# Attention's first loads and looks inside the last projections, and DVE alone for the sums of weights in the short sequence

## The chip, the core and the metric

The kernel runs on one core of a Trainium2 chip. The metric is the device time of one launch in microseconds, taken over several runs; beside it stands one execution taken by the hardware profiler, from which all rows of the profile come. TensorE is PE (its weight loads PEld), VectorE is DVE, ScalarE is ACT, GpSimd is POOL, and SyncE is SP. In this kernel SP issues every transfer.

## The reference

Two sequences, "prompt" with 1024 tokens and "sample" with 2048, go through one layer with shared weights. Everything is float32.

```python
h = rms_norm(x, norm_pre)
z = jnp.einsum('btd,de->bte', h, w_in)                    # 1024 -> 2304 columns
u_pool, g_pool, q, k, v, g_attn, q_x, g_x = jnp.split(z, SPLITS, axis=-1)
pool_out = multiscale_pool(u_pool, pool_w, pool_scale) * silu(g_pool)   # windows 2, 4, 8, 16
q = apply_rope(rms_norm(q, q_norm)); k = apply_rope(rms_norm(k, k_norm))
attn_out = block_self_attention(q, k, v) * silu(g_attn)   # 8 heads on 2 key heads, softmax over all tokens
k_m, v_m = split(rms_norm(mem, mem_norm) @ w_mem_kv)      # 256 memory tokens
x_out = memory_attention(q_x, k_m, v_m) * silu(g_x)       # 4 heads
y = concatenate([pool_out, attn_out, x_out]) @ w_out      # 1024 -> 1024
out = x + rms_norm(y, norm_post)
```

## The kernel before

**Phase 1, the projections.** `SB` lists what is projected: the memory, then the tokens in pieces of 1024 (two blocks of 512). For each piece six groups of weight columns run one after the other: queries (`group_n0`), a group of transposed chunks (`ct[2]`), queries, keys and values (`group_n1`), then three more groups of chunks, `ct[0]` (two pooling chunks and a gate), `ct[1]` (three gates) and `ct[3]` (a cross query and two gates). A product in float32 precision is made of three matmuls of high and low halves (L139 to L141, tile `pz`), eight times over the 1024 inputs, so 24 matmuls a tile. Results are staged in SBUF and stored to scratch in HBM: `dq`, `dqx` (queries), `dk`, `dv`, `dkm`, `dvm` (keys and values), `dg` (gates), `dp` (pooled input). A pooling chunk (`pool_chunk`) is windowed on POOL (tiles `s2`, `s4`, `sm`), multiplied with `poolw` on PE (`pm`, L332), scaled on DVE into `s4` again (L334), and stored from `s4` to `dp`. There is one `s4`, so the next chunk's second window sum, which writes it, waits for that store.

**Phase 2, the attention.** A pair is 256 queries; the 8 pairs of "sample" come first, then the 4 of "prompt". A pair has three groups: two of self-attention (kind 0 and 1, over 16 or 8 chunks of 128 keys) and one of cross-attention (kind 2, two chunks). The work is written out as a list of slots, one for each chunk of each group, and the order on PE, ACT, DVE and POOL is that of this program; SP's order is left to the scheduler. In a slot stand:

- `weights`: scores `S` of the chunk for two halves of the lanes (L595, L599: keys `KA` with query `qa`, then `KB` with `qb`, whose 65th row carries minus the maximum), and exp on ACT into `P` (L602).
- `sums`: adds the previous chunk's `P` into `z`, columns 0 to 511 on POOL, 512 to 1023 on DVE (L613, `CUT` = 512).
- `largest`, here called a look: scores `N` of 128 queries against up to 1024 keys (L567, L559), and a maximum over them on DVE (L570), for a group that starts at least four slots later. `N` has two buffers. After a group's last look, `shift` transposes the maxima (L504) and stores them as the row of `qb` (L584).
- `values`: every four chunks, `acc` += `P` times `V` (L625). After a group's last chunk `totals` multiplies `z` with a tile of ones in four quarters (L633), `take` multiplies `acc` with the gate, `inverse` takes the reciprocal (L645) and spreads it over partitions through HBM (`rows`, `gz`).
- `store_mix` multiplies (POOL, L661) and splits into high and low half (`mix`; ACT and POOL, L784); `Output.piece` is the output projection (L726 to L728, tile `py`, for the last pair `N`), spread over the next pair's slots. `Output.out` multiplies with the norm (L752) and adds the residual `xr` (L755). `xr` and `y` have one buffer each.

Since nothing of the first groups has been looked at when phase 2 begins, 20 looks stand ahead of its first slot: 16 of the second group, 2 of the first (cross-attention), 2 of the third. All tiles of phase 2 are taken when those of phase 1 have been given back.

Of the kernel before, what the change touches and what calls it, by code (L numbers as in the profile page):

```python
# [23 lines left out]
def encoder(ctx, tc, I, O):  # L24
# [46 lines left out]

    with ExitStack() as p1:
# [3 lines left out]
        pst = p1.enter_context(tc.tile_pool(name="pst", bufs=2, space=PSUM))  # L76
# [15 lines left out]
        def hT_block(sb, blk):  # L92
# [4 lines left out]
            for i in range(4):  # L97
                x = two.tile([128, D], F32, name="x", tag="x", bufs=4)
                nc.sync.dma_start(out=x, in_=rows(sb, blk, i))
                if kind not in gains:  # L100
                    gains[kind] = one.tile([128, D], F32, name="gain", tag="gain")
                    src = I["mem_norm" if kind == "mem" else "norm_pre"]
                    nc.sync.dma_start(out=gains[kind], in_=src.broadcast_to([128, D]))
                junk = one.tile([128, D], mybir.dt.bfloat16, name="junk", tag="junk")
                ss = two.tile([128, 1], F32, name="ss", tag="ss")
                nc.scalar.activation(out=junk, in_=x, func=AF.Square, accum_out=ss)
                r = rsqrt(two, ss, 1, D, "rsx")
# [27 lines left out]
        def product(ps, terms):  # L135

            n = len(terms)
            for c, (sh, sl, mh, ml) in enumerate(terms):
                nc.tensor.matmul(ps, lhsT=sh, rhs=mh, start=c == 0, stop=False)  # L139
                nc.tensor.matmul(ps, lhsT=sh, rhs=ml, start=False, stop=False)  # L140
                nc.tensor.matmul(ps, lhsT=sl, rhs=mh, start=False, stop=c == n - 1)  # L141

# [9 lines left out]
        def transposed(hT, w, col):  # L152

            ps = psz.tile([128, 512], F32, name="pz", tag="pz")
            f = slice(col, col + 128)
            product(ps, [(w[0][:, c, f], w[1][:, c, f], hT[0][:, c], hT[1][:, c]) for c in range(NC)])
            return ps
# [4 lines left out]
        def rope_tables():  # L162
            out = []
            raw = [two.tile([128, NTT, 64], F32, name="ropec", tag="ropec", bufs=1),
                   two.tile([128, NTT, 64], F32, name="ropes", tag="ropes", bufs=1)]
            for r, key in zip(raw, ("rope_c", "rope_s")):
                nc.sync.dma_start(out=r, in_=I[key])
            for key in ("k_norm", "q_norm"):
                g = one.tile([128, 2, 64], F32, name="hg", tag="hg" + key)
# [9 lines left out]
                for j in range(2):  # L179
                    if key == "q_norm":  # L180
                        t = raw[j]
                    else:
                        t = one.tile([128, NTT, 64], F32, name="ropek", tag=f"ropek{j}")
# [7 lines left out]
        def norm_rope(ps, parts, tt):  # L191
# [3 lines left out]
            z = two.tile([128, 384], F32, name="z", tag="z")  # L195
            sq = two.tile([128, 384], F32, name="sq", tag="sq")
            t1 = two.tile([128, 384], F32, name="t1", tag="t1")
            nc.scalar.copy(out=z[:, 0:w], in_=ps[:, 0:w])
            nc.scalar.activation(out=sq[:, 0:w], in_=ps[:, 0:w], func=AF.Square)
            ss = two.tile([128, 6], F32, name="ssh", tag="ssh")  # L200
# [3 lines left out]
            r = rsqrt(two, ss[:, 0:n], n, 64, f"rsh{n}")  # L204
# [22 lines left out]
        def heads_transposed(src, npair):  # L227
# [4 lines left out]
            o = two.tile([128, 2, 3, 128], F32R, name="qst", tag="qst")  # L232
# [20 lines left out]
        def group_n1(s, b, hT, w):  # L253
            for i in range(4):
                tt = 4 * b + i
                ps = natural(hT, w, i, 0, 384)
                vst = two.tile([128, 2, 64], F32, name="vst", tag="vst")
# [104 lines left out]
        def chunks_group(chunks):  # L362
            def run(s, b, hT, w):
                for k, (_, f, args) in enumerate(chunks):
                    f(s, b, *args, transposed(hT, w, 128 * k))
# [25 lines left out]
        def mem_v(s, b, hT, w):  # L391
            for i in range(4):
                ps = natural(hT, w, i, 0, 256).rearrange("p (h d) -> p h d", d=64)
                vst = two.tile([128, 4, 64], F32, name="vmst", tag="vmst", bufs=1)
# [15 lines left out]

        for sb, (kind, s, nb, b0) in enumerate(SB):
            groups = groups_of(sb)
            nxt = []
            for gi, (src, pieces, run) in enumerate(groups):
# [15 lines left out]
    with ExitStack() as p2:  # L430
        def pool(name, bufs, space=bass.MemoryType.SB):
            return p2.enter_context(tc.tile_pool(name=name, bufs=bufs, space=space, reuse_waits="tile"))

        one = pool("p2one", 1)
        two = pool("p2two", 2)
        pss = pool("pss", 2, PSUM)
        psn = pool("psn", 2, PSUM)
        psa = pool("psa", 1, PSUM)
        pso = pool("pso", 1, PSUM)

        ones = one.tile([128, 32], F32, name="ones")
        nc.vector.memset(ones, 1.0)

        KA = [one.tile([128, 2048], F32R, name=f"KA{kind}") for kind in range(2)]
        KB = [one.tile([128, 2048], F32R, name=f"KB{kind}") for kind in range(2)]
        KA.append(one.tile([128, 2, 2, NMEM], F32R, name="KA2"))
        KB.append(one.tile([128, 2, 2, NMEM], F32R, name="KB2"))
        for t in KB:  # L450
            nc.vector.memset(t[64:65].bitcast(F32), 1.0)
        V = [one.tile([128, 16, 64], F32, name=f"V{kind}") for kind in range(2)]
        V.append(one.tile([128, 2, 4, 64], F32, name="V2"))
        has_K, has_V = set(), set()

        def load_K(s, kind):
            has_K.add((s, kind))
            for hl in range(2):
                for t, h in ((KA, 64 * hl), (KB, 0))[:2 - hl]:
                    if kind == 2:  # L460
                        src = DKM[hl, :, :, s].rearrange("d (c j) m -> d c j m", j=2)
                        nc.sync.dma_start(out=t[2][h:h + 64].bitcast(F32), in_=src)
                        continue
                    for a in range(0, SEQS[s][1], 1024):
                        nc.sync.dma_start(out=t[kind][h:h + 64, a:a + 1024].bitcast(F32),
                                          in_=DK[s][kind][hl, :, a:a + 1024])

        def load_V(s, kind):
            has_V.add((s, kind))
            if kind == 2:  # L470
                nc.sync.dma_start(out=V[2], in_=DVM[s])
                return
            for a in range(0, SEQS[s][1] // 128, 8):
                nc.sync.dma_start(out=V[kind][:, a:a + 8], in_=DV[s][kind][:, a:a + 8])

        wo_hi = one.tile([128, NC, D], F32R, name="wo_hi")
        wo_lo = one.tile([128, NC, D], F32R, name="wo_lo")
        raws = {}

        def load_w_out(c):  # L480
            raws[c] = two.tile([128, D], F32, name="raw", tag=("y", "xr")[c % 2], bufs=1)
            nc.sync.dma_start(out=raws[c], in_=I["w_out"][0, 128 * c:128 * c + 128])

        def split_w_out(c):
            raw = raws.pop(c)
            nc.scalar.copy(out=wo_hi[:, c], in_=raw)
            nc.gpsimd.tensor_tensor(out=wo_lo[:, c], in0=raw, in1=wo_hi[:, c].bitcast(F32), op=ALU.subtract)

        npost = one.tile([128, D], F32, name="npost")

        def load_npost():
            nc.sync.dma_start(out=npost, in_=I["norm_post"].broadcast_to([128, D]))


        lanes32 = {}
        for name in ("top",):
            lanes32[name] = [one.tile([128, 32], F32, name=f"{name}{n}") for n in range(2)]
            for t in lanes32[name]:
                nc.vector.memset(t, 0.0)

        def lanes_to_rows(t, name):

            r = two.tile([128, 32], F32, name="rows32", tag=f"r{name}")
            nc.vector.transpose(out=r, in_=t)  # L504
            return r

        BASE = (2, 4, 6)

        class Group:

            def __init__(self, n, s, p, kind):
                self.n, self.s, self.p, self.kind = n, s, p, kind
                T = SEQS[s][1]
                self.chunks = 2 if kind == 2 else T // 128
                self.parts = 1 if kind == 2 else T // 1024
                self.pieces = [(0, j) for j in range(2)] if kind == 2 else \
                    [(a, lane) for a in range(self.parts) for lane in range(8)]
                self.P = {}  # L520

            def load(self):
                s, p, kind = self.s, self.p, self.kind
                if (s, kind) not in has_K:
                    load_K(s, kind)
                self.qa = one.tile([128, 2, 512], F32R, name="qa", tag="qa", bufs=4)
                for h in range(2):
                    self.load_q(self.qa[64 * h:64 * h + 64], 0)
                self.top = lanes32["top"][self.n % 2]
                if self.parts > 1:  # L530
                    self.nb = two.tile([128, self.parts, 8], F32, name="nb", tag="nb")

            def load_q(self, out, hl):
                s, p = self.s, self.p
                src = DQX[s, p // 2][hl, p % 2].rearrange("d j c q -> d j (c q)") if self.kind == 2 else \
                    DQ[s, p, self.kind][hl].rearrange("d j t i q -> d j (t i q)")
# [221 lines left out]

        CUT = 512


# [156 lines left out]
```

## Time and profile before

| | |
|---|---|
| median of 3 runs | 1941.95 us (1940.56 to 1943.42) |
| profiled execution | 1940.45 us, span 1938.6 us |
| granted TensorE clock, mean | 0.974 |
| PE / DVE / POOL / ACT busy | 1830.0 / 1126.4 / 914.3 / 699.3 us |
| phase 1, first to last projection matmul | up to 691.8 us |
| first score matmul | 746.2 us |
| short sequence's sums | about 1608 to 1895 us |

A busy engine isn't always at its peak, so what a stage waits for is read from the rows: a timeline row gives the start, the length, the engine and line, what is written from what, how often, and in brackets the idle time before it with the event that ended it. A row of the chain of waits gives start, length and what held the end. A row of waits gives who waited for whom: total, times, longest.

### The profile page before, as it was taken

The numbers are of one execution on the slowest core, as the hardware profiler recorded it, in microseconds if no ns is written. First come the engines' busy times: TensorE is split into PE (matmuls) and PEld (weight loads), VectorE is DVE, ScalarE is ACT, GpSimd is POOL, SyncE is SP. The second block draws the span as 40 slices with busy tenths as digits, with TensorE's granted clock in tenths as the row PEclk, the third lists the DMA queues.
The fourth block names the chain that finished last, engine by engine and source line by source line (L and its number), as shares of the span: only waits on it lengthen the run. The fifth ranks groups of instructions, "written<-read, shape, count | busy, mean of one in ns | idle before, by whom it ended". The sixth has DMA issues, their size and how long they took to land.

```text
span 1938.6 us, 23683 instructions
## 1 busy us (share of the span) xinstructions
PE 1830.0 (94%) x8520; PEld 1289.7 (67%) x8520; DVE 1126.4 (58%) x1304; ACT 699.3 (36%) x1266; POOL 914.3 (47%) x816
## 2 busy tenths in 40 slices
PE   7999999999999938999999999999999999999995
PEld 6998898978998824456565655656565655565564
DVE  6833254422623018876767677676767666756742
ACT  5522242313422102543434444443434443333331
POOL 3735033620634003863746456373746454635644
PEclk9999999999999967899999999999999999999998
DMA  6653355434443273212112021222212143323211
GB/s 235 200 147 89 110 161 138 116 100 123 118 123 86 66 176 118 82 39 77 60 47 80 26 79 44 77 60 77 61 48 78 49 125 83 93 77 104 82 39 60
DMA packets 148486, 181.84 MB, mean 94 GB/s; under 512 B 21504, under 2 KB 118416, under 8 KB 148368
## 3 DMA queue, kind: packets, MB, share of 16 engines
q1 hardware_dynamic: 148368, 180.33, 32.6%
q8 instruction: 67, 1.10, 0.2%
q14 instruction: 51, 0.42, 0.1%
HBM read 126.50 MB, written 53.62 MB: 93 GB/s over the span
## 4 chain that ended last, share of the span: by engine, by line
PE 70%; issue 10%; DVE 8%; POOL 6%; DMA 4%; ACT 2%; SPq 1%; POOLq 0%; ACTq 0%; DVEq 0%
PE acc L625 13%; PE S L595 11%; PE pz L141 9%; PE pz L139 9%; PE pz L140 9%; PE N L567 6%; PE py L726 3%; PE py L727 3%; PE py L728 3%; DVE nb L570 2%; POOL z L613 2%; DVE z L613 2%; PE S L599 1%; POOL rs L63 1%; PE N L633 1%
## 5 line engine op out<-in xcount | busy, mean ns | idle before, releaser
L602 ACT ACTIVATE P<-S 128x512 f32<-128x512 f32 x688 | 401.3, 599 | 612.8 <-PE S L595 435.4
L613 POOL TENSOR_TENSOR z<-z,P 128x512 f32<-128x512 f32 x272 | 389.2, 1431 | 260.3 <-ACT P L602 253.9
L570 DVE TENSOR_REDUCE nb<-N 128x1 f32<-128x1024 f32 x256 | 311.0, 1218 | 229.0 <-PE N L567 228.2
L625 PE MATMUL acc<-P,V 128*64 128x512 f32 (+1 forms) x1472 | 318.2, 574 | 0.5
L595 PE MATMUL S<-qa,KA 128*128 128x512 f32 x640 | 277.3, 433 | 11.6 <-ACT P L602 11.5
L613 DVE TENSOR_TENSOR z<-z,P 128x512 f32<-128x512 f32 x272 | 262.2, 964 | 15.9 <-ACT P L602 15.4
L567 PE MATMUL N<-KA,qa 128*128 128x512 f32 x640 | 217.0, 423 | 46.1 <-DMA qa<-dq 29.5
L595 PE MATMUL S<-qb,KB 65*128 65x512 f32 x640 | 255.2, 399 | 0.0
L139 PE MATMUL pz<-hT_hi,w_hi 128*128 128x512 f32 x592 | 233.2, 394 | 2.6 <-ACT w_hi L68 1.8
L140 PE MATMUL pz<-hT_lo,w_hi 128*128 128x512 f32 x592 | 233.9, 395 | 0.0
L141 PE MATMUL pz<-hT_hi,w_lo 128*128 128x512 f32 x592 | 232.3, 392 | 0.0
L595 PEld LDWEIGHTS S<-qa,KA 128*128 128x128 f32 x640 | 121.7, 190 | 146.4 <-issue 71.9
L625 PEld LDWEIGHTS acc<-P,V 128*64 128x64 f32 x1472 | 98.1, 137 | 177.6 <-issue 168.5
L567 PEld LDWEIGHTS N<-KA,qa 128*128 128x128 f32 x640 | 119.3, 198 | 97.5 <-DVE nb L570 35.1
L63 POOL TENSOR_TENSOR rs<-rs,mhalf 128x1 f32<-128x1 f32 (+2 forms) x100 | 92.9, 932 | 175.7 <-DVE rs L61 175.5
L570 DVE TENSOR_REDUCE top<-N 128x1 f32<-128x1024 f32 (+1 forms) x88 | 107.1, 1218 | 109.5 <-PE N L567 79.6
L613 POOL TENSOR_TENSOR z<-P 128x512 f32<-128x512 f32 x36 | 46.6, 1294 | 215.4 <-ACT P L602 154.3
L140 PE MATMUL pz<-w_lo,hT_hi 128*128 128x384 f32 (+1 forms) x416 | 140.5, 338 | 0.9 <-DVE w_lo L69 0.8
L141 PE MATMUL pz<-w_hi,hT_lo 128*128 128x384 f32 (+1 forms) x416 | 140.2, 338 | 0.0
L139 PE MATMUL pz<-w_hi,hT_hi 128*128 128x384 f32 (+1 forms) x416 | 139.4, 336 | 0.0
L726 PE MATMUL py<-wo_hi,mix 128*128 128x512 f32 x352 | 138.0, 392 | 0.0
L727 PE MATMUL py<-wo_lo,mix 128*128 128x512 f32 x352 | 137.2, 390 | 0.0
(115 smaller groups left out, 2587.5 us busy)
## 6 DMA issues: line engine op xcount, KB each, us to landing
wraw<-w_in SPq DMA_DIRECT2D x15, 1536.0 KB
dg<-gst SPq DMA_DIRECT2D x48, 256.0 KB
qa<-dq SPq DMA_DIRECT2D x48, 256.0 KB
gz<-rows SPq DMA_DIRECT2D x72, 128.0 KB
x<-x_sample SPq DMA_DIRECT2D x16, 512.0 KB
xr<-x_sample SPq DMA_DIRECT2D x16, 512.0 KB
y_sample<-xr SPq DMA_DIRECT2D x16, 512.0 KB
dq<-qst SPq DMA_DIRECT2D x48, 128.0 KB
```

Source lines behind the costliest of these rows:

```text
L63: nc.gpsimd.tensor_tensor(out=r, in0=r, in1=mhalf[:, 0:n], op=ALU.pow)
L139: nc.tensor.matmul(ps, lhsT=sh, rhs=mh, start=c == 0, stop=False)
L140: nc.tensor.matmul(ps, lhsT=sh, rhs=ml, start=False, stop=False)
L141: nc.tensor.matmul(ps, lhsT=sl, rhs=mh, start=False, stop=c == n - 1)
L567: nc.tensor.matmul(S[:, 512 * b:512 * b + 512], lhsT=q, rhs=KA[self.kind][:, k:k + 512], start=True, stop=True)
L570: nc.vector.tensor_reduce(out=out, in_=S, axis=AX.X, op=ALU.max, negate=True)
L595: nc.tensor.matmul(S, lhsT=K[self.kind][rows_, keys], rhs=q, start=n == 0, stop=n == 1)
L602: nc.scalar.activation(out=self.P[k][:, j], in_=S, func=AF.Exp)
L613: e.tensor_tensor(out=z[:, x], in0=a[:, x], in1=P[:, x], op=ALU.add)
L625: nc.tensor.matmul(self.acc[64 * j:64 * j + 64, x], lhsT=v, rhs=P[:, j, x], start=(k, i) == (0, 0), stop=k == self.chunks - 1, skip_group_ ...
L726: nc.tensor.matmul(ps, lhsT=mh, rhs=wo_hi[:, c, cols], start=first, stop=False)
L727: nc.tensor.matmul(ps, lhsT=mh, rhs=wo_lo[:, c, cols], start=False, stop=False)
```

## The change

Three things change. The diff below is cut to them; most of the other changed lines only move the classes of phase 2 ahead of phase 1 and rename pools (`one` and `two` of phase 2 are now `own` and `dbl`; those tiles of phase 1 that aren't needed in its last three groups are in `fone` and `ftwo`, on the other side of SBUF). The quarters of ones in `totals` are the same in both.

1. After `group_n1` of the last piece, `fone` and `ftwo` are given back, and `early` takes their room: `KA`, two of three `KB`, queries, maxima. The first three groups are loaded there (`load`). After `ct[0]` the PSUM banks of phase 1's transposes go to `N`. In the last group (`ct[3]`) one look is written behind every second of a product's eight steps; PE's order is by hand there. `KB` is now loaded in `shift`, and `KB1` stays in the late pool.
2. `CUT` is 512 for "sample" and 0 for "prompt": there DVE adds all 1024 columns in one instruction, and POOL none.
3. In the last pair, `xr` and `y` of both tiles take buffers of `P` and are loaded before the first product.

```diff
+    def look_ahead():
+        if ahead:
+            g, n = ahead.pop(0)
+            g.largest(n)
...
-        def product(ps, terms):
+        def product(ps, terms, beside=lambda: None):
...
+                if c % 2:
+                    beside()
...
+                last = sb + 1 == len(SB)
+                if last and gi == 3:
+                    front.close()
+                    early = ctx.enter_context(tc.tile_pool(name="early", bufs=1, side="right", reuse_waits="tile"))
+                    open_early()
+                    for g in loads.pop(-1):
+                        g.load()
+                if last and gi == 4:
+                    heads.close()
+                    psn = ctx.enter_context(tc.tile_pool(name="psn", bufs=2, space=PSUM, side="right", reuse_waits="tile"))
...
-                    run(s, b0 + blk, cur[blk], w)
+                    if last and final:
+                        with tc.manual_schedule(engines={mybir.EngineType.PE}):
+                            run(s, b0 + blk, cur[blk], w, look_ahead)
+                    else:
+                        run(s, b0 + blk, cur[blk], w)
...
-            with tc.high_priority(offset=2000):
-                for g in loads.pop(-1):
-                    g.load()
-                for g, n in ahead:
-                    g.largest(n)
...
             def shift(self):
+            load_K(self.s, self.kind, KB, 0, 0)
...
-                for e, x in ((nc.gpsimd, slice(0, CUT)), (nc.vector, slice(CUT, 1024))):
-                    e.tensor_tensor(out=z[:, x], in0=a[:, x], in1=P[:, x], op=ALU.add)
+            cut = CUT[self.s]
+            if cut:
+                nc.gpsimd.tensor_tensor(out=z[:, :cut], in0=a[:, :cut], in1=P[:, :cut], op=ALU.add)
+            nc.vector.tensor_tensor(out=z[:, cut:], in0=a[:, cut:], in1=P[:, cut:], op=ALU.add)
...
-        CUT = 512
+    CUT = (0, 512)
...
-                self.xr = two.tile([128, D], F32, name="xr", tag="xr", bufs=1)
+            tag = dict(tag="P", bufs=6) if self.last else dict(tag="xr", bufs=1)
+            self.xr = dbl.tile([128, D], F32, name="xr", **tag)
...
                 if self.last:
                     if self.both is None:
+                    self.start()
```

How the order moves, first on SP, in the last piece between `group_n1` and the pooling chunks' stores. Before (`dk` keys, `dp` pooled input, `dg` a gate):

```order
L237 DMA dk_114<-qst 64x2x128
L338 DMA dp_112<-s_5394 128x512
L343 DMA dg_2_0_98<-gst 512x1x128
L338 DMA dp_112<-s_5433 128x512
L343 DMA dg_3_0_107<-gst 512x1x128
L338 DMA dp_112<-s_5503 128x520
```

And now (KA_5378, KA_5379, KA_5376 are the keys of kind 1, 2 and 0, KB_... their second copies):

```order
L648 DMA dk_114<-qst 64x2x128
L99 DMA KA_5378<-dk_114 64x1024 x4
L161 DMA qa<-dq_0_1_76 64x1024 x2
L96 DMA KA_5379<-dkm 64x4x256 x2
L161 DMA qa<-dqx_0_79 64x1024 x2
L99 DMA KA_5376<-dk_114 64x1024 x4
L161 DMA qa<-dq_0_0_75 64x1024 x2
L749 DMA dp_112<-s_5437 128x512
L754 DMA dg_2_0_98<-gst 512x1x128
L96 DMA KB_5380<-dkm 64x4x256
L161 DMA qb<-dqx_0_79 64x1024
L99 DMA KB_5377<-dk_114 64x1024 x2
```

Sixteen loads stand between the last store of keys and the first store of the pooled input, nine more behind it; before, all of them stood behind the last gate of phase 1.

On PE, the second pooling product `pm` of the same stage, before, at the start of the gate tile of `ct[0]`'s second block:

```order
L141 MATMUL pz_5517<-hT_hi_4214,w_lo_4906 128x512
L139 MATMUL pz_5563<-hT_hi_4214,w_hi_4905 128x512
L140 MATMUL pz_5563<-hT_lo_4215,w_hi_4905 128x512
L332 MATMUL pm_5441<-sm_5434,poolw_145 128x512
L141 MATMUL pz_5563<-hT_hi_4214,w_lo_4906 128x512
```

And now, in the second gate tile of `ct[1]`:

```order
L550 MATMUL pz_5672<-hT_hi_4038,w_lo_5366 128x512
L548 MATMUL pz_5672<-hT_hi_4038,w_hi_5365 128x512
L549 MATMUL pz_5672<-hT_lo_4039,w_hi_5365 128x512
L743 MATMUL pm_5484<-sm_5477,poolw_151 128x512
L550 MATMUL pz_5672<-hT_hi_4038,w_lo_5366 128x512
```

It stands 54 projection matmuls later than before.

On PE at the seam, before, from the last projection matmul to the first scores:

```order
L141 MATMUL pz<-hT_hi,w_lo 128x512
L567 MATMUL N<-KA_5966,qa 128x512 x28
L559 MATMUL N<-KA_5970,qa 128x256 x8
L567 MATMUL N<-KA_5966,qa 128x512 x4
L567 MATMUL N<-KA_5967,qa 128x512 x4
L599 MATMUL S<-qa,KA_5970 128x256 x2
L599 MATMUL S<-qb,KB_5971 128x256 x2
```

And now, first a place in the last projection group, then the seam itself:

```order
L191 MATMUL N<-KA_5376,qa 128x512 x2
L548 MATMUL pz<-hT_hi,w_hi 128x512
L549 MATMUL pz<-hT_lo,w_hi 128x512
L550 MATMUL pz<-hT_hi,w_lo 128x512
L548 MATMUL pz<-hT_hi,w_hi 128x512
L549 MATMUL pz<-hT_lo,w_hi 128x512
L550 MATMUL pz<-hT_hi,w_lo 128x512
L191 MATMUL N<-KA_5376,qa 128x512 x2
```

```order
L550 MATMUL pz<-hT_hi,w_lo 128x512
L224 MATMUL S<-qa,KA_5379 128x256 x2
L224 MATMUL S<-qb,KB_5380 128x256 x2
L191 MATMUL N<-KA_5378,qa 128x512 x2
L224 MATMUL S<-qa,KA_5379 128x256 x2
```

The 20 looks lie in the first five of the last group's six tiles; nothing but scores follows the last projection matmul.

More of the change, by code (lines that the diff above doesn't have):

```diff
@@ new lines, in due, with open_fill @@
+    def due(slot):
+        for f, args in later.pop(slot, ()):
+            f(*args)
+    first = {}
+    for n, (g, k) in enumerate(slots):
+        first.setdefault(g, n)
+    fill, until = [], [0]
+    def open_fill(pair, slot):
+        fill.extend(pair.todo())
+        n = pairs.index(pair) + 1
+        until[0] = first[pairs[n].groups[0]] + HOLD[pairs[n].s] if n < len(pairs) else slot
+    for pair in pairs:
+        ends = [first[g] + g.chunks - 1 for g in pair.groups]
+        at(min(ends), pair.load_pool)
+        free = 0 if pair is pairs[0] else first[pair.groups[0]] + HOLD[pair.s]
+        at(max(min(ends) + 4, free), pair.pool, max(min(ends) + 4, free))
+        for g in pair.groups:
+            wait = max(first[g] + g.chunks + 5, free)
+            at(wait + END, g.mix_out, wait + END, pair)
+        at(max(ends) + 9, open_fill, pair, max(ends) + 9)
@@ new lines, in encoder @@
+    for g in groups:
+        n, c = first[g], g.chunks
+        at(n + END, g.load_late)
+        for k in range(0, c, RUN):
+            ks = list(range(k, min(k + RUN, c)))
+            at(n + ks[-1] + 1 + END, g.values, ks)
+        at(n + c + 1 + END, g.totals)
+        at(n + c + 2, g.take)
+        at(n + c + 2 + END, g.inverse)
+    for c in range(NC):
+        at(4 + 3 * c, load_w_out, c)
+        at(7 + 3 * c, split_w_out, c)
+    at(7 + 3 * NC, load_npost)
+    looks, n = {}, len(slots)
@@ new lines, in encoder @@
+    left = {g: list(range(len(g.pieces))) for g in groups}
+    while any(left.values()):
+        n -= 1
+        able = [g for g in groups if left[g] and first[g] - LEAD > n]
+        if able:
+            looks[n] = (able[0], left[able[0]].pop())
+    ahead = [looks[n] for n in sorted(looks) if n < 0]
+    loads = {}
+    for n, (g, k) in looks.items():
+        if k == 0:
+            loads.setdefault(max(n - 3, -1), []).append(g)
+    order = {mybir.EngineType.PE, mybir.EngineType.Activation, mybir.EngineType.DVE,
+             mybir.EngineType.Pool}
@@ L182, in rope_tables @@
                     else:
-                        t = one.tile([128, NTT, 64], F32, name="ropek", tag=f"ropek{j}")
+                        t = fone.tile([128, NTT, 64], F32, name="ropek", tag=f"ropek{j}")
                     nc.gpsimd.tensor_tensor(out=t, in0=raw[j],
@@ new lines, in encoder @@
+    V.append(own.tile([128, 2, 4, 64], F32, name="V2"))
+    wo_hi = own.tile([128, NC, D], F32R, name="wo_hi")
+    wo_lo = own.tile([128, NC, D], F32R, name="wo_lo")
+    npost = own.tile([128, D], F32, name="npost")
+    with tc.manual_schedule(engines=order):
+        slot = 0
+        while slot < len(slots) or later or fill:
+            g, k = slots[slot] if slot < len(slots) else (None, 0)
+            if g:
+                g.weights(k, 0)
+            if 0 < slot <= len(slots):
+                h, kh = slots[slot - 1]
+                h.sums(kh)
+            for x in loads.get(slot, ()):
+                x.load()
+            if slot in looks:
+                looks[slot][0].largest(looks[slot][1])
+            due(slot)
+            if g:
+                g.weights(k, 1)
+            pauses = sum(x is None for x in fill)
+            n = -(-(len(fill) - pauses) // max(1, until[0] - slot - pauses)) if fill else 0
+            for _ in range(n):
+                x = fill.pop(0)
+                if x is None:
+                    break
+                out, h, c, start, final = x
+                out.piece(h, c, start, final)
+                if final:
+                    if h == 0 and not out.last:
+                        for n in sorted(later):
+                            for x in [x for x in later[n] if x[0].__name__ in ("square", "norm", "out")]:
+                                later[n].remove(x)
+                                x[0](*x[1])
+                    at(slot + END, out.half_out, h)
+                    at(slot + 1 + END, out.square, h)
+                    if h == 1:
+                        at(slot + 2, out.norm)
+                        at(slot + 3, out.out)
+            due(slot + END)
+            slot += 1
```

690 lines of the change are left out of this document (305 added, 385 removed).

## The prediction

> **What bounds the kernel now.** I read the page's slices of time first, then the windows by stage, the chain of waits at the seam between the two phases, and last the waits of PE in the short sequence and at the end. In the windows the columns after the stage and its length are the busy time (and count) of PE, PEld, DVE, ACT and POOL, then PE's granted clock, the DMA engines' share and GB/s.
>
> ```profile
> PE   7999999999999938999999999999999999999995
> 600.00:691.80 91.80, 91.77 (x400) 74.25 (x399) 17.31 (x23) 12.57 (x18) 12.78 (x13) 1.00 0.23 70
> 691.80:721.20 29.40, 0.00 (x0) 0.00 (x0) 0.00 (x0) 1.88 (x2) 0.00 (x0) 0.55 0.98 207
> 721.20:746.20 25.00, 23.03 (x44) 11.38 (x45) 22.34 (x22) 0.00 (x0) 0.00 (x0) 0.50 0.68 198
> 1730.00:1810.00 80.00, 75.38 (x346) 49.47 (x347) 50.68 (x53) 29.71 (x57) 43.11 (x30) 0.98 0.34 98
> ```
>
> PE is the bound nearly everywhere; the "3" in its slices is the seam. There PE does nothing for 29.4 us while the DMA engines are 98% busy, and then works at half its clock (0.50) for 25 us. In the 91.8 us before, PE is full, DVE has 17 us of work and the DMA engines are 77% free.
>
> ```profile
> 691.54 0.24 PE pz L141
> 711.46 9.73 DMA qa<-dq
> 721.23 1.24 PE N L567 x2
> 722.49 1.24 DVE nb L570
> 746.24 0.63 PE L599 MATMUL S<-qa,KA 128*128 128x256 f32 x2
> 751.06 0.63 PE L567 MATMUL N<-KA,qa 128*128 128x512 f32 x2
> 751.53 0.40 PE L595 MATMUL S<-qa,KA 128*128 128x512 f32 x1
> 752.09 1.95 PE L625 MATMUL acc<-P,V 128*64 128x256 f32 x16
> 693.07 1.27 SPq L465 DMA_DIRECT2D KA<-dk  x2
> 686.42 0.60 ACT L342 ACTIVATE gst<-pz 128x512 f32<-128x512 f32 x1 [4.90 <-PE pz L141]
> 691.86 0.60 ACT L342 ACTIVATE gst<-pz 128x512 f32<-128x512 f32 x1 [4.84 <-PE pz L141]
> 692.47 1.28 ACT L602 ACT_TABLE_LOAD   x1
> 747.73 0.60 ACT L602 ACTIVATE P<-S 128x512 f32<-128x512 f32 x1 [53.97 <-PE S L599]
> ```
>
> The last projection matmul ends at 691.78, and the first score matmul of the attention starts at 746.24: 54.5 us. 29.5 of them go to loads, 25.0 to 20 looks (products for the maxima, each with one reduction), in which PE and DVE take turns at 1.24 us each. Later, between other work, a look holds PE for 0.47 us (751.06 to 751.53). A projection matmul takes 0.227 us: a tile has 24 of them, and two tiles' ACT rows lie 5.44 us apart. The load queue's pace: 21 loads of 256 KB from 693.07 to 711.46 + 9.73 = 721.19, that is 1.34 us each; I take 1.4 under a full queue.
>
> **The seam.** All 54.5 us go. What comes back:
> The 20 looks in the last projections: 20 x 0.47 = 9.4 us of PE. Each has the time of six projection matmuls beside it, 6 x 0.227 + 0.47 = 1.8 us, and DVE needs 1.24, so DVE doesn't hold PE up. The row of maxima for the first group leaves after the 16th look and has two projection tiles' time, 11 us, to land.
> At the seam itself: the last gate (0.60) and the table load (1.28) now stand ahead of the first exponential, which can start about 1.95 us after the last projection; before, it started 1.49 us (746.24 to 747.73) after the first score. DVE has two memsets there. Values and gates can only be loaded now, because the projections' tiles hold their room. The first values are third on the queue, behind the last gate stores: 0.6 + 3 x 1.4 = 4.8 us after the last projection, against a first use 5.85 us after the first score (752.09). That is just in time. On the other side the half-speed matmuls behind the pause end. Together between -1.5 us (only the speed-up counts) and +4 us (values or gates late by three loads); I take +1, since the rows say just in time. Term: -54.5 + 9.4 + 1.0 = -44.1 us.
>
> **The loads at their new place.** The new order puts 16 loads on SP's queue between the last store of keys and the first store of the pooling result.
>
> ```profile
> 606.47 0.34 SPq L338 DMA_DIRECT2D dp<-s  x1
> 608.74 1.06 POOL L304 TENSOR_TENSOR s<-s 128x525 f32<-128x525 f32 x1 [6.48 <-DMA dp<-s]
> 612.81 0.75 DVE L325 SCALAR_TENSOR_TENSOR sm<-sm,invw,u 128x512 f32<-128x512 f32 x1 [1.41 <-POOL sm L304]
> 618.24 1.03 PE L332 MATMUL pm<-sm,poolw 128*128 128x512 f32 x2
> ```
>
> POOL waits for that store (dp), because the next pooling chunk writes the tile it is stored from; 4.8 us after it, at 613.56, sm is ready, and PE takes it at 618.24. Now the store is the 17th: it lands at 606.5 + 17 x 1.4 = 630.3 instead of 608.74, and sm is ready at 635.1. The new order has PE take it 54 matmuls later than before, at 618.24 + 54 x 0.227 = 630.5. PE works in order, so it stops for 4.6 us, and loses 1.4 more to the clock (next part): +6 us. Bounds: 0, if loads start before the last keys are stored and the store overtakes part of them; +10, if they start 2 us later and the gate stores, now behind nine more loads, stop ACT for a while. The looks don't wait: their keys land by about 629, the first look comes at about 666.
>
> **DVE alone in the short sequence.** 60 POOL adds go, and 60 DVE adds become twice as wide.
>
> ```profile
> PE N L633 <- POOL z L613: 10.4, 4, 3.2
> 1681.22 1.08 PE L633 MATMUL N<-z,ones 128*32 128x256 f32 x8 [3.23 <-POOL z L613]
> 1755.62 0.76 PE L633 MATMUL N<-z,ones 128*32 128x256 f32 x8 [3.23 <-POOL z L613]
> 1758.19 0.63 PE L595 MATMUL S<-qa,KA 128*128 128x512 f32 x1
> 1758.62 0.63 PE L595 MATMUL S<-qb,KB 65*128 65x512 f32 x1
> 1748.69 1.75 DVE L613 TENSOR_TENSOR z<-z,P 128x512 f32<-128x512 f32 x1
> 1751.55 2.35 POOL L755 TENSOR_TENSOR xr<-xr,y 128x1024 f32<-128x1024 f32 x1
> 1766.55 0.68 DVE L613 TENSOR_TENSOR z<-z,P 128x512 f32<-128x512 f32 x1
> 557.12 3.36 DVE L69 TENSOR_TENSOR w_lo<-wraw,w_hi 128x3072 fp32r<-128x3072 f32 x1 [17.58 <-ACT w_hi L68]
> L613 DVE TENSOR_TENSOR z<-z,P 128x512 f32<-128x512 f32 x61 | 65.5, 1074 | 11.5 <-ACT P L602 11.2
> ```
>
> Four times PE waits for POOL's sum of weights: three pairs lose 3.23 us each, because POOL's add stands behind a residual sum of 2.35 us; the rest, 0.7 us, belongs to a group of the long sequence and stays. After each stop matmuls come 0.43 us apart (1758.19, 1758.62) instead of 0.227, for some 3.8 us: a loss of 0 to 1.9 us, and I count 1.4. The 1024-wide add costs 0.68 + 512 x (3.36 - 0.68)/2560 = 1.22 us, against 1.07 in the mean now, where POOL disturbs the narrow ones (up to 1.75): 60 x 0.15 = 9 us more of DVE over four pairs of 74.4 us (1681.22 to 1755.62). DVE is busy for 50.68 of 80 us there, so the rest covers most of it; in the slots without output projection, though, DVE has an add and a look each while PE has little more, and I charge 0.6 us a pair. Term: -3 x (3.23 + 1.4 - 0.6) = -12 us; bounds -14 (nothing charged) and 0 (DVE late by as much as POOL was).
>
> The Trainium skill, page "SBUF — State Buffer", section "Who interferes with whom", says that a DVE instruction with two SBUF inputs and a GpSimd instruction that reads SBUF exclude each other, and the later one waits until the earlier has finished. The 1.75 beside the 0.68 us agrees. The same notes, page "TensorE: Matmul & The Clock Gate", section "What's actually happening", let the clock fall to half behind an idle window of about 3.4 us. Here 3.23 us were enough. Taken by its letter the rule would strike 1.4 us from each of three stops, and the sum would come out 4.2 us higher.
>
> The copies of keys for the second operand (KB) are now loaded when a group's last look is out; that is four slots ahead, with the DMA engines 34% busy: 0, at most 1 us for each of three.
>
> **The end.** The last pair's residual tiles and results get buffers of their own, and the residuals are loaded before the products.
>
> ```profile
> 1899.65 0.65 PE L633 MATMUL N<-z,ones 128*32 128x256 f32 x4 [6.58 <-POOL z L613]
> 1891.00 2.29 DVE L752 SCALAR_TENSOR_TENSOR y<-y,rs,npost 128x1024 f32<-128x1024 f32 x1 [0.45 <-POOL rs L63]
> 1890.94 3.47 POOL L661 TENSOR_TENSOR o<-o,gz 128x512 f32<-128x512 f32 x2
> 1899.56 1.26 POOL L784 TENSOR_TENSOR mix<-pu,mix 128x512 fp32r<-128x512 f32 x1
> 1901.68 0.63 PE L728 MATMUL N<-wo_hi,mix 128*128 128x512 f32 x1
> 1930.38 3.21 DMA xr<-x_prompt
> 1928.24 1.41 DVE L752 SCALAR_TENSOR_TENSOR y<-N,rs,npost 128x512 f32<-128x512 f32 x2
> 1933.70 1.77 POOL L755 TENSOR_TENSOR xr<-xr,y 128x512 f32<-128x512 f32 x1 [6.12 <-DMA xr<-x_prompt]
> ```
>
> PE's wait of 6.58 us for POOL ends. Late next: DVE's own last add, behind the 2.29 us product (1893.3 + 1.22 = 1894.5 for the totals), and POOL's mix<-pu, which L728 needs. If POOL starts its two o products at 1890.94 as before, a residual sum (2.35) and mix (1.26) end at 1898.0 instead of 1900.82; without the adds ahead of them the o products may start some 2 us earlier too. So 3 to 5 us, and 1 to 1.5 for the shorter stop's clock: -5 (-3 to -6.5). On SP's queue the new residual loads stand ahead of the last rows of totals, but wait only for weights' tiles that are used up by then: 0.
> At the very end the second tile's residual (1930.38 to 1933.59) could only be loaded when the first tile had been stored. Now its sums follow DVE's products, done at 1929.65, and end near 1930.6 instead of 1933.70 + 1.77 = 1935.47: -5 (-4 to -5.5).
>
> **Sum.** -44.1 + 6 - 12 - 5 - 5 = -60.1 us. The profiled execution took 1940.45 us (1938.6 of them the span), so 1880.3; it lies 1.5 us under the median of 1941.95, so I forecast 1881 us, between the two.
>
> **Rivals.** A: the pooling store lands in time and PE doesn't stop there: 1881 - 6 = 1875. The 23% of DMA use there speaks for it, the 98% at 207 GB/s during these very loads against it.
> B: in the short sequence DVE takes POOL's place as the bound. POOL's residual sums and mix products lengthen the wide adds by 1.75 - 0.68 = 1.07 us each; on some seven adds of a pair's tight slots that is 7.5 us, of which the 4.6 us of the stop that went cover a part. The 12 us don't come, and up to 3 x 3 more are lost: 1893 to 1902. Against it: the mean of 1.07 us now holds such delays already, with twice the POOL work. By the port rule of the skill, B is what the change invites.
> C: values or gates come late at the seam by one round of the queue, 6 loads x 1.4 = 8 us: 1889. For it: gate stores, values, gates and pooled inputs all start at the seam; against it: 4.8 against 5.85 us.
> D, not faster: DVE alone is so slow that all gains go. A pair's DVE work is 50.68/80 x 74.4 = 47 us; less 15 x 1.07, plus 15 x d for the wide add, it would have to fill 70 + 60/4 = 85 us a pair: d = 3.6 us. Twice the longest narrow add is 3.5.
> E: the looks still stand behind the projections because their loads come late. The new order and the 37 us of slack (629 to 666) all but exclude it; half of the first 29 us would come back, 1895 or more.
>
> **Chances.** Forecast (1877 to 1887) 0.53, A 0.17, B 0.14, C 0.11, D 0.02, E 0.03. The range reaches from A with the other terms at their better ends (1870) to the nearer half of B and most of E (1896). A measurement of this kernel tells about 0.2% (4 us) from no change; all cases but D lie far under it: faster 0.98, same 0.01, slower 0.01.
>
> **What would show it.** Right: no PE gap over 3 us between the last pz and the first S; N matmuls about 1.8 us apart among the last pz; one PE wait of 3 to 7 us at the pooling's second pm, behind dp; z of 128x1024 at 1.2 to 1.4 us; no wait of PE for POOL's z in the short sequence; the last two xr loaded before their products. Wrong: a stop of over 5 us at the first acc matmuls (C); DVE over 85% busy in the short sequence, with PE waiting for N's or rz's readers (B).

## The result, and the profile after

The changed kernel takes 1898.59 us (median of 4 runs, 1897.63 to 1901.11) against 1941.49 before (four runs now): a ratio of 0.978, 95% interval 0.9763 to 0.9797. That is 42.9 us faster; 60 were forecast, and the time lies 2.6 us above the range. The profiled execution has a span of 1896.4 us.

Rows that mark the stages, first of before, then of after: ACT's first gate of the pooling stage, its first exponential (before: 747.73, shown above), PE's totals of the last long group, and its totals of the last group but one.

```profile
607.08 0.60 ACT L342 ACTIVATE gst<-pz 128x512 f32<-128x512 f32 x1 [5.11 <-PE pz L141]
1607.87 0.64 PE L633 MATMUL N<-z,ones 128*32 128x256 f32 x8 [0.68 <-POOL z L613]
1866.34 0.64 PE L633 MATMUL N<-z,ones 128*32 128x256 f32 x8
```

```profile
605.11 0.60 ACT L753 ACTIVATE gst<-pz 128x512 f32<-128x512 f32 x1 [5.08 <-PE pz L550]
706.46 1.09 ACT L227 ACTIVATE P<-S 128x512 f32<-128x512 f32 x2
1569.91 0.64 PE L260 MATMUL N<-z,ones 128*32 128x256 f32 x8 [0.66 <-POOL z L239]
1830.43 0.64 PE L260 MATMUL N<-z,ones 128*32 128x256 f32 x8
```

| stage | before, us | after, us | difference | forecast |
|---|---|---|---|---|
| up to the pooling stage's first gate | 607.08 | 605.11 | -2.0 | 0 |
| to the first exponential (pooling, looks, seam) | 140.65 | 101.35 | -39.3 | -38.1 |
| to the last long group's totals (long sequence) | 860.14 | 863.45 | +3.3 | 0 |
| to the totals of the last group but one (short sequence) | 258.47 | 260.52 | +2.05 | -12 |
| to the end | 72.26 | 65.97 | -6.3 | -10 |
| sum | 1938.6 | 1896.4 | -42.2 | -60.1 |

The first row is no effect of the change: in the profiles of the experiments this anchor lies anywhere from 603.47 to 606.77, and at 604.63 in experiment 2, whose first phase is that of the kernel before. The difference in the seam came as forecast. Behind it 21 us are missing: 14 in the short sequence, 3.3 in the long one, 3.7 at the end; the first two rows make up for 3 of them.

**The seam.** The slices of PE have lost their "3", and the windows (columns as in the prediction) of the last 33 us of projections and of the 15 us behind them show it:

```profile
PE   7999999999999998999999999999999999999996
672.00:705.00 33.00, 33.00 (x151) 27.44 (x150) 19.95 (x20) 2.83 (x5) 0.00 (x0) 1.00 0.22 51
705.00:720.00 15.00, 12.82 (x70) 8.32 (x68) 12.60 (x13) 8.81 (x15) 6.79 (x6) 1.00 0.83 249
704.07 0.40 PE L550 MATMUL pz<-hT_hi,w_lo 128*128 128x512 f32 x1
704.31 0.40 PE L224 MATMUL S<-qa,KA 128*128 128x256 f32 x2
```

PE is full with the looks among the projections, the first score follows the last projection at once, and the clock stays at 1.00 (it was 0.50 for 25 us).

**The pooling store.** POOL waits for `dp`, sm is late, and PE stops, as forecast (3.33 us; 4.6 were forecast):

```profile
617.40 0.33 SPq L749 DMA_DIRECT2D dp<-s  x1
626.13 1.06 POOL L715 TENSOR_TENSOR s<-s 128x525 f32<-128x525 f32 x1 [25.82 <-DMA dp<-s]
631.99 2.04 PE L743 MATMUL pm<-sm,poolw 128*128 128x512 f32 x2 [3.33 <-DVE sm L736]
```

From the first gate to the last one takes 99.4 us (605.11 to 704.55), against 84.8 before (607.08 to 691.86) plus 9.4 for the looks: the stop costs 5.3 us if the looks cost what was forecast; 6 were forecast.

**A longer stop in the long sequence.** PE, ACT, POOL and SP behind the seam:

```profile
736.40 0.80 PE L220 MATMUL S<-qa,KA 128*128 128x512 f32 x1 [5.42 <-ACT P L227]
737.55 5.38 PE L252 MATMUL acc<-P,V 128*64 128x512 f32 x16
735.23 0.62 ACT L416 CAST mix<-o 128x512 fp32r<-128x512 f32 x1 [6.72 <-POOL o L288]
733.94 1.26 POOL L288 TENSOR_TENSOR o<-o,gz 128x512 f32<-128x512 f32 x1 [3.75 <-DMA gz<-rows]
724.99 0.55 SPq L274 DMA_DIRECT2D rows<-rz  x1
730.41 1.10 SPq L278 DMA_DIRECT2D gz<-rows  x2
```

And the same place before:

```profile
775.06 0.50 PE L595 MATMUL S<-qa,KA 128*128 128x512 f32 x1 [2.14 <-ACT P L602]
773.89 0.62 ACT L784 CAST mix<-o 128x512 fp32r<-128x512 f32 x1 [3.43 <-POOL o L661]
```

The first group's inverse totals go to HBM at 724.99 and are asked back only at 730.41, when they have landed, behind the values, the rows of w_out, the second keys and npost that start at the seam now. POOL waits for them, ACT stands in order behind POOL with a copy that nobody needs yet, its exponentials stand behind the copy, and PE behind those. The 16 value matmuls after the stop take 5.38 us; in most places they take 3.65. The stop isn't new, though: before, PE stopped at the same matmul for 2.14 us, and the value matmuls behind it took 5.35. There the totals' round trip was short (`rows` at 761.20, `gz` asked back at 762.95, with the DMA engines 38% busy), and POOL waited for nobody; it was late by its own work, a split of w_out and a mix product. What is new is POOL's wait of 3.75 us for `gz`: ACT's wait grew by 3.29 us, PE's by 3.28, and the whole long sequence by 3.3.

**The short sequence.** PE's wait for POOL's sum is gone. What stands at the border of two pairs now, on PE, DVE and POOL:

```profile
1714.33 0.64 PE L260 MATMUL N<-z,ones 128*32 128x256 f32 x8 [0.33 <-DVE top L194]
1721.36 1.22 PE L191 MATMUL N<-KA,qa 128*128 128x512 f32 x2 [1.96 <-DVE rz L272]
1723.36 5.70 PE L252 MATMUL acc<-P,V 128*64 128x512 f32 x16
1710.85 2.29 DVE L240 TENSOR_TENSOR z<-z,P 128x1024 f32<-128x1024 f32 x1
1715.33 1.21 DVE L240 TENSOR_TENSOR z<-P 128x1024 f32<-128x1024 f32 x1
1718.94 0.69 DVE L266 TENSOR_TENSOR o<-acc,gate 128x512 f32<-128x512 f32 x1 [1.27 <-POOL mix L416]
1719.55 1.75 DVE L272 RECIPROCAL rz<-N 128x256 f32<-128x256 f32 x1
1712.02 3.35 POOL L386 TENSOR_TENSOR xr<-xr,y 128x1024 f32<-128x1024 f32 x1
1715.33 2.35 POOL L416 TENSOR_TENSOR mix<-pu,mix 128x512 fp32r<-128x512 f32 x1
1717.64 2.51 POOL L416 TENSOR_TENSOR mix<-o,mix 128x512 fp32r<-128x512 f32 x2
1721.00:1725.00 4.00, 3.65 (x8) 1.69 (x10) 3.96 (x6) 0.60 (x1) 0.00 (x0) 0.50 0.59 198
PE N L191 <- DVE rz L272: 6.5, 4, 2.0
```

The next look needs the `N` buffer that holds the totals, so it waits for the reciprocal; DVE's reciprocal stands behind the take; and the take writes an `o` tile (two buffers) that POOL still reads for the last pair's mix (the first of the two `mix<-o,mix` at 1717.64). POOL is late because its residual sum takes 3.35 us (2.35 before) and its mix product 2.35 (1.27 before, in the row at 1755.53 of that trace): beside a DVE add of 1024 columns each waits for the other, and the add takes 2.29 where it is 1.21 alone. Two adds a pair are lengthened like that (in the next one 2.02 and 2.29 us, at 1764.40 and 1785.93), and DVE is busy for 50.36 of the 75 us from 1714 to 1789. PE stops for 1.96 us, and the clock falls to 0.50. The last line is the waits' row for 1570 to 1896: four stops, 6.5 us (three of them 1.96); before, this wait was 1.2 us there.

### The profile page after: what moved, and what is told of

It is laid out like the page before. It is cut to its first block, busy times and chain, and to the rows that moved or that the text cites. A ratio compares the mean times of both kernels' runs of the same rounds, so it can differ in the third digit from the quotient of the medians.

```text
span 1896.4 us, 23574 instructions
## 1 busy us (share of the span) xinstructions
PE 1821.4 (96%) x8520; PEld 1283.3 (68%) x8520; DVE 1140.7 (60%) x1304; ACT 696.8 (37%) x1266; POOL 838.6 (44%) x756
## 5 line engine op out<-in xcount | busy, mean ns | idle before, releaser
L239 POOL TENSOR_TENSOR z<-z,P 128x512 f32<-128x512 f32 x224 | 316.3, 1412 | 225.1 <-ACT P L227 220.2
L252 PE MATMUL acc<-P,V 128*64 128x512 f32 (+1 forms) x1472 | 323.9, 583 | 0.5
L240 DVE TENSOR_TENSOR z<-z,P 128x512 f32<-128x512 f32 (+1 forms) x272 | 277.2, 1019 | 17.4 <-ACT P L227 16.8
L191 PE MATMUL N<-KA,qa 128*128 128x512 f32 x640 | 208.1, 407 | 20.5 <-DVE rz L272 11.9
L357 PE MATMUL py<-wo_hi,mix 128*128 128x512 f32 x352 | 137.7, 391 | 0.0
L359 PE MATMUL py<-wo_hi,mix 128*128 128x512 f32 x352 | 137.3, 390 | 0.0
```

What stands on the lines that cost most here:

```text
L191: nc.tensor.matmul(S[:, 512 * b:512 * b + 512], lhsT=q, rhs=KA[self.kind][:, k:k + 512], start=True, stop=True)
L239: nc.gpsimd.tensor_tensor(out=z[:, :cut], in0=a[:, :cut], in1=P[:, :cut], op=ALU.add)
L240: nc.vector.tensor_tensor(out=z[:, cut:], in0=a[:, cut:], in1=P[:, cut:], op=ALU.add)
L252: nc.tensor.matmul(self.acc[64 * j:64 * j + 64, x], lhsT=v, rhs=P[:, j, x], start=(k, i) == (0, 0), stop=k == self.chunks - 1, skip_group_ ...
L357: nc.tensor.matmul(ps, lhsT=mh, rhs=wo_hi[:, c, cols], start=first, stop=False)
```

## The experiments

Ten kernels, each against runs of the kernel before on the same chip (medians 1940.95, 1941.59 and 1941.4).

**1. POOL's half back in the short sequence** (changed kernel).

```diff
-    CUT = (0, 512)
+    CUT = (512, 512)
```

> The changed kernel with one part undone: in the short sequence POOL adds the first 512 columns of the weights' sum again. Theory 1 (the prediction's third term: DVE alone takes three stops of 4.6 us off PE, and part of the stop at the end): the stops come back, 12 to 15 us more than the changed kernel's 1898.6, about 1911 to 1913. Theory 2 (the stop only moved: with wide adds DVE reaches the reciprocal late, behind POOL's products that the adds themselves lengthen, and PE stops at the next look instead): a pair takes 74.0 to 74.4 us in place of 75.07, and the four pairs give back what the end loses, so 1896 to 1901, no difference that counts.

Measured: 1900.6 us, ratio 0.9794 (0.9778 to 0.9811), against 0.978 with the change: no difference that is clear of the noise (the intervals overlap). The short sequence takes 258.2 us (1572.93 to 1831.17), the three stops of 3.24 us are back. The end takes 67.73 us in place of 65.97. Theory 1, my third term, fell.

**2. DVE alone, and nothing else of the change** (kernel before).

```diff
-  for e, x in ((nc.gpsimd, slice(0, CUT)), (nc.vector, slice(CUT, 1024))):
+  for e, x in ((nc.gpsimd, slice(0, CUT)), (nc.vector, slice(CUT, 1024))) if self.s else ((nc.vector, slice(0, 1024)),):
```

> The kernel before with one part of the change alone: DVE adds all 1024 columns in the short sequence. Theory 1: 12 us faster than before, 1929.5. Theory 2 (the stop moves from the totals to the look behind them): 1939 to 1942, no difference; the trace shows no wait of PE for POOL's sums, and instead waits of 1.5 to 2 us for the reciprocal once in each pair.

Measured: 1939.78 us, ratio 0.9998 (0.9988 to 1.0007). From the other side the same: this part is worth nothing on its own. The wait moved as said:

```profile
PE N L567 <- DVE rz L645: 6.5, 4, 2.0
PE N L633 <- DVE z L613: 1.4, 1, 1.4
```

**3. The first group's mix four slots later** (changed kernel).

```diff
-            wait = max(first[g] + g.chunks + 5, free)
+            wait = max(first[g] + g.chunks + (9 if g is groups[0] else 5), free)
```

> The changed kernel, with the first group's product by its inverse totals (POOL) and the copy into mix (ACT) placed four slots later; the loads stay. Theory 'row behind the loads' (POOL waits for the inverse totals' round trip through a queue that moves 231 GB/s, ACT stands in order behind POOL, and PE behind ACT): the stop of 5.42 us at 736.40 and its half-speed matmuls (1.6 us) go: 1891.5 us, 6 to 7.5 less than 1898.6. Rival (ACT would stop there anyway, for w_out's rows or the keys, since everything on the queue is late): a stop of 3 us or more stays within 10 us of that place, and the time within 3 us of 1898.6.

Measured: 1890.92 us, ratio 0.9743 (0.9729 to 0.9758): 7.7 less. The inverse totals are just as late (rows at 725.30, gz at 730.25), but POOL takes them later and waits for nothing, and PE's longest wait there is 1.78 us:

```profile
739.02 1.76 POOL L288 TENSOR_TENSOR o<-o,gz 128x512 f32<-128x512 f32 x1
741.98 0.50 PE L220 MATMUL S<-qa,KA 128*128 128x512 f32 x1 [1.78 <-ACT P L227]
```

So what stops PE is not the loads as such, but ACT, which takes its work in the program's order, behind a result that the loads had delayed. The long sequence takes 856.9 us (706.08 to 1562.98), 3.2 less than before the change: the edit also takes away most of the price of the 2.14 us stop that stood there already. Most of the gain over the kernel before, 2.4 us, lies between the first group's totals and the second's (44.72 us against 47.08).

**4. The early loads one group of projections later** (changed kernel).

```diff
                     open_early()
-                    for g in loads.pop(-1):
-                        g.load()
                 if last and gi == 4:
+                    for g in loads.pop(-1):
+                        g.load()
                     heads.close()
```

> The changed kernel, with the early loads issued one group of projections later in the program; the queue's order then has the first pooling store behind one load instead of sixteen, and PE takes the second pooling matmul at its old place. Theory of the prediction's second term (the stop at the second pooling matmul is the store behind the loads): the stop of 3.33 us at 631.99 and about 1.5 us of half-speed matmuls go, 1893 to 1895. Rival (the loads are only pushed into a place where they hurt as much: the third and fourth pooling matmuls stop behind their stores, or the looks wait for keys): within 3 us of 1898.6.

Measured: 1892.56 us (1888.1 to 1899.17), ratio 0.9757 (0.9733 to 0.9782), 6.0 less; the runs lie far apart and the profiled one was the slowest, so I read the stage and not the span. First gate to last gate takes 96.1 us (606.46 to 702.57) in place of 99.4: 3.3 of the 5.3 us. The second pooling matmul comes without a stop; the last one now waits for its own store:

```profile
618.29 1.02 PE L743 MATMUL pm<-sm,poolw 128*128 128x512 f32 x2
639.46 1.09 POOL L715 TENSOR_TENSOR s<-s 128x541 f32<-128x541 f32 x1 [16.56 <-DMA dp<-s]
644.68 1.25 PE L743 MATMUL pm<-sm,poolw 128*128 128x512 f32 x4 [1.56 <-DVE sm L736]
```

Both were partly right: the store behind the loads is the cause, and a part of it was only pushed on. The stage is 11.3 us longer than before; less the stop of 1.56 us, that leaves 9.8 us for the 20 looks, where 9.4 were forecast.

**5. POOL's residual sum nearly left out in the short sequence** (changed kernel; the last pair keeps it).

```diff
-  (nc.vector if h else nc.gpsimd).tensor_tensor(out=x[:, c], in0=x[:, c], in1=y[:, c], op=ALU.add)
+  d = slice(0, 64) if s == 0 and not self.last else c
+  (nc.vector if h else nc.gpsimd).tensor_tensor(out=x[:, d], in0=x[:, d], in1=y[:, d], op=ALU.add)
```

> The changed kernel without 15/16 of POOL's residual sums in the first three pairs of the short sequence (64 of 1024 columns are added, the rest is left out); DVE's instructions stay. Theory 'POOL's chain' (the take waits for POOL, which is late by its residual sum of 2.35 to 3.35 us, and that sum and DVE's wide adds lengthen each other): the add of 2.29 us falls to 1.22, the take's wait of 1.27 us goes, PE's three stops of 2.9 us with their half-speed matmuls go for the most part, and the stop at the end shrinks: 12 to 17 us less, 1882 to 1887. Rival 'DVE's own work' (wide adds and reductions one behind the other are simply too long for these slots): 3 to 5 us less, 1893 to 1896.

**6. DVE's adds half as wide** (changed kernel; each group's first add stays wide, and adds 1.0 so that no total is zero).

```diff
-  cut = CUT[self.s]
-  if cut:
+  cut = 512 if self.s == 0 and k > 1 else CUT[self.s]
+  if self.s:
...
```

> The changed kernel with DVE's adds in the short sequence cut to 512 columns except each group's first (half of the sum is left out, POOL adds nothing); all else stays. Theory 'DVE's own work': the stops of the short sequence go, 10 to 15 us less, 1884 to 1888, as the prediction's third term had it. Theory 'POOL's chain': the take still waits for POOL, so a narrower add brings 0.5 to 1.5 us a pair and about 1 at the end: 1893 to 1897.

Measured: experiment 5 takes 1885.68 us, ratio 0.9711 (0.9695 to 0.9727), and experiment 6 takes 1886.01 us, ratio 0.9715 (0.9701 to 0.973). Both leave out work, so their times tell who holds whom and aren't times of the whole job. The fifth came as 'POOL's chain' said, the sixth as 'DVE's own work' said: 12.6 us below the changed kernel, where POOL's chain gave 2 to 6. They are not rivals. Experiment 5 carries its own control: at the first border of pairs POOL still sums the last long pair's residual in full, and there the take's wait and the stop remain, while at the later two the take waits for nobody and the stop is 0.59 and 0.58 us. The rows of the first border:

```profile
1646.43 0.69 DVE L266 TENSOR_TENSOR o<-acc,gate 128x512 f32<-128x512 f32 x1 [1.28 <-POOL mix L417]
1648.84 1.22 PE L191 MATMUL N<-KA,qa 128*128 128x512 f32 x2 [1.97 <-DVE rz L272]
```

With narrow adds POOL gets through sooner too, and the take waits for nobody (rows of experiment 6):

```profile
1705.41 2.83 POOL L386 TENSOR_TENSOR xr<-xr,y 128x1024 f32<-128x1024 f32 x1
1708.20 1.27 POOL L416 TENSOR_TENSOR mix<-pu,mix 128x512 fp32r<-128x512 f32 x1
1711.72 0.69 DVE L266 TENSOR_TENSOR o<-acc,gate 128x512 f32<-128x512 f32 x1
```

The Trainium skill, page "SBUF — State Buffer", section "Who interferes with whom", has a DVE instruction with two SBUF inputs contend with a GpSimd instruction that reads SBUF. The trace agrees in both directions: DVE's add 2.29 against 1.21 us, POOL's mix product 2.35 against 1.27.

**7. Four buffers for gates and products** (changed kernel): the take waits for POOL no more, and no work changes.

```diff
-  self.gate = dbl.tile([128, 2, 2, 128], F32, name="gate", tag="gate")
+  self.gate = dbl.tile([128, 2, 2, 128], F32, name="gate", tag="gate", bufs=4)
...
-  self.o = dbl.tile([128, 512], F32, name="o", tag="o")
+  self.o = self.gate.rearrange("p i t q -> p (i t q)")
   nc.vector.tensor_tensor(out=self.o, in0=self.acc,
-                          in1=self.gate.rearrange("p i t q -> p (i t q)"), op=ALU.mult)
+                          in1=self.o, op=ALU.mult)
```

> The changed kernel, where the product of values and gates is written over the gates, which have four buffers now in place of two, so that the take no longer needs a tile that POOL still reads; no work is added or left out. Theory 'POOL's chain through the buffer of o': the take starts 1.27 us earlier, the stop of 1.96 us at the look behind it falls below 1 us and its half-speed matmuls go: 2 to 3.3 us a pair, 1889 to 1893. Rival (the take waits for the port, or DVE is late anyway): within 3 us of 1898.6, with the take still idle for over 1 us.

Measured: 1890.86 us, ratio 0.9742 (0.9728 to 0.9757): 7.7 less. The add still takes 2.29 us and POOL's residual sum 3.35, but the take doesn't wait, the stop at the look is 0.58 or 0.59 us, and the clock holds:

```profile
1711.26 2.29 DVE L240 TENSOR_TENSOR z<-z,P 128x1024 f32<-128x1024 f32 x1
1718.00 0.68 DVE L266 TENSOR_TENSOR gate<-acc,gate 128x512 f32<-128x512 f32 x1
1648.76 0.73 PE L191 MATMUL N<-KA,qa 128*128 128x512 f32 x2 [0.58 <-DVE rz L272]
1720.00:1728.00 8.00, 7.61 (x32) 3.80 (x33) 7.93 (x10) 2.74 (x5) 0.56 (x1) 1.00 0.57 183
```

The short sequence takes 251.2 us (1572.59 to 1823.80), 9.3 less than with the change alone.

**8. Edits 3, 4 and 7 together.**

> Three edits together: the first group's mix four slots later, the early loads one group of projections later, four buffers for gates and products. If they add up: 1898.6 less 7.7 (measured), less about 3.3 (the part of the pooling stop that went by the trace), less 6 to 10 (if the buffer theory holds): 1878 to 1882. If the buffers bring nothing: 1886 to 1889.

Measured: 1880.54 us, ratio 0.9688 (0.9674 to 0.9702). They add up, with the 3.3 us that the stage of experiment 4 showed; with that run's 6.0 the sum would have been 1877.

**9. POOL's half back in version 8** (`CUT = (512, 512)`).

> The version with the three edits (1880.5 us), with POOL's half of the weights' sums in the short sequence put back. Theory 'the third term was right but for the buffer' (DVE alone is worth 7 us in the first three pairs once the take waits for nobody): the short sequence's first three pairs take 258 us again in place of 251.0, the stops of 3.23 us behind POOL's sum are back, and the end costs about 2 more: 1887 to 1891. Rival (the four buffers alone brought the gain, whoever adds): 1880 to 1883.

Measured: 1891.17 us, ratio 0.9741 (0.9727 to 0.9754): 10.6 more. The short sequence takes 259.6 us (1564.46 to 1824.06) against 251.0 (1563.58 to 1814.62), with PE's stop back:

```profile
1711.33 1.08 PE L260 MATMUL N<-z,ones 128*32 128x256 f32 x8 [3.23 <-POOL z L239]
```

So DVE alone is worth 8.6 us there once the take is free; the rest is at the end, which takes 69.1 us in place of 65.7 in these two profiles.

**10. Version 8 with the last but one pair's second tile finished four slots later.** After the change the end looked like this on DVE, POOL and PE:

```profile
1855.98 2.28 DVE L240 TENSOR_TENSOR z<-z,P 128x1024 f32<-128x1024 f32 x1
1853.10 4.09 POOL L288 TENSOR_TENSOR o<-o,gz 128x512 f32<-128x512 f32 x2
1857.15 3.34 POOL L386 TENSOR_TENSOR xr<-xr,y 128x1024 f32<-128x1024 f32 x1
1858.32 0.64 PE L260 MATMUL N<-z,ones 128*32 128x256 f32 x8 [1.39 <-DVE z L240]
1861.76 0.79 PE L359 MATMUL N<-wo_hi,mix 128*128 128x512 f32 x1 [2.14 <-POOL mix L416]
```

```diff
-                        at(slot + 3, out.out)
+                        at(slot + (7 if out.pair is pairs[-2] else 3), out.out)
```

> The version with the three edits, with the last but one pair's second tile finished four slots later (DVE's product behind the last take and reciprocal, POOL's residual sum behind the last mix products). Theory 'at the end POOL's residual sum and DVE's product, each lengthened by the other, hold the totals and the mix': the waits of 1.39 us for DVE's sum and 2.14 us for POOL's mix go, with the half-speed matmuls behind them; without that residual sum the way from the totals to the end was 33.45 us in place of 38.08: 4.5 to 6 us less, 1874 to 1876. Rival (the inverse totals come later in turn, or PE stops for the last group's mix instead): within 2 us of 1880.5.

Measured: 1875.11 us (1874.22 to 1880.66), ratio 0.9668 (0.9652 to 0.9683), 5.4 less and the best of all. The totals no longer wait for DVE's sum, PE waits for the mix for 0.44 us at most, and the residual sum (now 2.39 us) stands behind the mix products:

```profile
1838.07 0.64 PE L260 MATMUL N<-z,ones 128*32 128x256 f32 x8
1839.59 3.51 POOL L416 TENSOR_TENSOR mix<-gate,mix 128x512 fp32r<-128x512 f32 x2
1843.06 2.39 POOL L386 TENSOR_TENSOR xr<-xr,y 128x1024 f32<-128x1024 f32 x1
```

## Why the prediction was right and wrong

- **Seam (-44.1) and pooling store (+6).** Together -38.1 against -39.3. The stop was 3.33 us at `pm`, about 5.3 in all, for the reason given, and experiment 4 shows the cause. The looks cost 9.8 us by that experiment, near the 9.4 forecast.
- **DVE alone (-12).** This term failed: +2 in its place. I charged 0.6 us a pair for DVE and looked only at who holds the totals. I did not follow DVE's next instructions: the take behind a tile that POOL reads, the reciprocal behind the take, the look behind the reciprocal. Once PE came 3 us earlier, that chain was the limit. Rival B, whose range of 1893 to 1902 holds the result, named DVE as the bound and the wide adds' lengthening as the price. The lengthening of one add was right (2.29 against 1.21), but two adds a pair have it and not seven, and DVE is busy for 67% of the time and not over 85%. B's other sign, PE's wait for the reader of `rz`, did come: the loss came through POOL and one buffer. Experiments 1, 2, 7 and 9 show it: the part is worth 0 without the buffer and 8.6 us with it. Even then it is less than 12, and in experiment 7 PE still stops three times at each border of two pairs, for 0.33 to 0.59 us each, at the totals and at two looks.
- **The long sequence (0).** The missing term. Rival C had late transfers behind the seam, but looked for them at values and gates, and at the first value matmuls. Those were in time; late was the round trip of the first inverse totals, and the step I missed is that ACT waits in order for POOL's result. Before, the same loads had 29 us of idle PE to land in. The stop there was 2.14 us before and is 5.42 now, so the term that I put at 0 measures +3.3. Experiment 3 brought 7.7 us (6.6 by that stage's length), more than the change had cost, because it took away the old part of the stop and its slow matmuls as well.
- **The end (-5 and -5).** The residual of the second tile came as forecast: with experiment 1, where the end differs from before by the early residual loads alone, it takes 67.73 us (1831.17 to 1898.9) in place of 72.26: -4.5. The totals' wait fell from 6.58 to 1.39 us, and I had the mix follow in time; instead POOL's two products took 4.09 us and its residual sum 3.34 beside DVE's wide adds, so PE stopped another 2.14 us and worked slowly behind it: -1.8 in place of -5. Experiment 10 got the rest: the end takes 60.8 us there against 65.7 in version 8.

## What to carry to other kernels

When a wait is taken away, follow the engine that now arrives early to its next few semaphores, and each of those back through the buffers it writes: the stop may move a few microseconds on and cost the same. When loads are moved out of a pause, list the small round trips that used that pause as well, and what stands in order behind whoever waits for them. An in-order engine should not be given a result that nobody needs yet while it may still be late; four slots were worth 7.7 us, 3.3 of which the change itself had cost.

## What was not expected of the hardware

After the change, each of the three stops of PE of 1.96 us was followed by a lower granted clock (0.69 in the 4 us behind the first, 0.50 behind the other two), and the next 16 value matmuls took 5.35, 5.70 and 5.71 us in place of 3.65. With stops of 0.58 us (experiment 7) the clock stayed at 1.00, so a stop 1.4 us shorter saved about 3 us a pair. But the length of one stop doesn't decide it alone. Behind the seam PE stops for 1.78 us at the same matmul in experiments 3 and 8: the clock stayed at 1.00 in the one, and was 0.71 in the other, with value matmuls of 5.35 us. And in experiment 6 stops of only 0.88 and 0.71 us, 2.4 us apart from start to start of the matmuls behind them, were followed by a clock of 0.50 (from 1714 to 1718) and value matmuls of 5.89 us. What decides between these cases stays open here.

The lengthening of DVE's and POOL's instructions beside each other works both ways by about the same, 1.0 to 1.1 us on each side.
